# A two-layer decoder trunk on one core: the next norm's weights applied after the transposes, two more pairs by seven products, fewer up blocks added by TensorE, and the issue order as a table

## The chip, the core and the metric

The kernel runs on 1 core of one Trainium2 chip. The metric is the device time of one execution in microseconds (us). Engines are called PE (TensorE), DVE (VectorE), ACT (ScalarE), POOL (GpSimd) and SP (the queue that issues most loads).

## The reference

Two layers over x of 256 tokens by 1024 columns, in float32. Each layer normalises x, projects it, runs two groups of attention heads, projects back, and adds the normalised result to x; then the same around an MLP with a squared ReLU:

```python
for l in range(DEPTH):
    h = _rms_norm(x, g_pre_mix[l])
    parts = jnp.split(h @ w_in[l], split_at, axis=-1)
    ...
    mix = jnp.concatenate([o_nsa, o_fox], axis=-1) @ w_out[l]
    x = x + _rms_norm(mix, g_post_mix[l])
    h = _rms_norm(x, g_pre_mlp[l])
    y = jnp.square(jax.nn.relu(h @ w_up[l])) @ w_down[l]
    x = x + _rms_norm(y, g_post_mlp[l])
```

`_rms_norm(x, g)` is x divided by the root of the mean of its squares in a row, times g by columns. `w_up` is 1024 by 4096, `w_down` 4096 by 1024. `o_nsa` is compressed, windowed and selected attention with gates, `o_fox` attention with forget gates.

## The kernel before

**Rounded products.** A float32 matrix is used as the sum of a high and a low part, both in a rounded float format (F32R) that PE streams at one column per cycle. A product of two matrices is three matmuls (`mm3`, line 811): high by high, high by low, low by high. The high half is a copy on ACT, the low half a difference on DVE (`split`, line 832; for weights `Weights.get`, line 567, and `Weights.pair`, line 614). Weight tiles of 512 KB are loaded on SP's queue into the tile wraw, their halves are whi and wlo; of each, seven buffers rotate (`WBUFS`, `LBUFS`, lines 53 and 55). Some up blocks have another way of splitting, by DMAs that POOL issues (`UPS`, line 57).

**The seams.** After attention and after the MLP, `sandwich` (line 883) closes a half layer for one token tile of 128 rows at a time: squares of the bank on ACT, the factor r (`rsqrt_sum`, line 836), the new x, and, in three of the four cases, the normed input of the next half layer, turned so that columns lie on partitions (`to_xT`, line 866: four transposes into one PSUM bank, then one split of 512 columns). Before, the next norm's weights g are applied by columns ahead of the transposes: `pre_gain` (line 874) makes xo = x g and the product of both weights; mg = bank times that product; mg r + xo, in four parts of 256 columns, is what is transposed. The new x itself is made afterwards (m = bank times g_post; x = m r + x). The weights lie in SBUF as rows copied to all partitions (`load_gains`, line 787, tiles gain0 and gain1). The row factor of the next norm is left out here and multiplied in later, as it is one number for each row.

**The MLP.** The hidden width is 32 blocks of 128. Up block 0 to 3 are made by token (`up0`, line 1672). The other 28 are made transposed, two to a step u, in a loop over u (line 1722). A block is one of two kinds. In `add_block` (line 1626) PE adds all three products into one half of a PSUM bank, 24 matmuls of 256 columns. In `up_block` (line 1616) each high weight multiplies the high and low input at once (`block_products`, line 818: 8 matmuls of 512 columns), the low weight 8 times 256; ACT copies the bank out as y, and DVE adds its halves into h. `SUMMED` (line 60) says for each step of a layer which kind its two blocks are: before, 13 of 14 steps of layer 0 and 11 of layer 1 add on PE.

The down product takes the hidden blocks in pairs, by `PAIRS` (line 65): "N" is a plain two by two block product (two token tiles by two column halves by two hidden blocks: eight products), "S" does it with seven products in the manner of Strassen, with sums of weight blocks (wsum) and of activation blocks (quads) made on DVE, into seven PSUM banks that are put together at the end of the layer. Before, 12 of 14 pairs of layer 0 and 14 of 15 of layer 1 are "S"; the remaining hidden blocks are multiplied plainly at the end (`down`, line 1782).

**The order of the work.** Nothing is issued as the program calls it. A `Recorder` (line 221) keeps every operation, works out dependences, and simulates the engines with costs, due times and buffer counts (`order`, line 326; `schedule`, line 356); then `emit` (line 474) issues the operations in that order, and each engine runs its own in it. 92 ranks found beforehand (`RANKS`, line 66) override the computed ones. All instructions are issued at line 481, so the profile tells them apart by tiles.

Of the kernel before, what the change touches and what calls it, by code (L numbers as in the profile page):

```python
# [18 lines left out]
F32 = mybir.dt.float32  # L19
# [15 lines left out]
LANE = 0.9  # L35
PASSES = 4
LANDING = 3500.0

ADDING, ADDED, CAST = 2600, (5000, 5000), (1870, 2500)
SLACK, LATE = {"vector": 20, "scalar": 20}, 1000  # L40

RAMP = {0: 900, 1: 420}
WAIT = 0.4
WARM = (256, 256, 256, 256, 128)
ENTER, LEAVE = 90, 200
SEQ = [(2, 0), (2, 1), (2, 2), (2, 3), (3, 0), (3, 1), (3, 2), (3, 3)]
EVKEY = 1
FIRSTS = [(k, k + 1) for k in range(8)]
NFIRST = 768
HOLD = 150  # L50
REACH = 40
UPK = 7
TOK, WBUFS, RBUFS = 6, 7, 9
LOAD_LEAD, SPLIT_LEAD, ADD_LEAD, CAST_LEAD = 12, 1, 5, 10
# [5 lines left out]
SUMMED = ("11101111111111", "11011111110101")  # L60
# [4 lines left out]
PAIRS = ("NSSSSSSSSSSSSN", "NSSSSSSSSSSSSSS")  # L65
RANKS = (
# [17 lines left out]
)  # L84
QT = (1, 1)
# [130 lines left out]
class Op:  # L216
    __slots__ = ("small", "engine", "name", "args", "kw", "key", "urgent", "cost", "deps", "succs", "bufs",
                 "missing", "ready", "start", "end", "tile", "rank")


class Recorder:
    def __init__(self, nc, tc):
        self.nc, self.tc = nc, tc
        self.ops, self.stages, self.fifo, self.key, self.hot, self.lane, self.group = [], [], {}, None, False, None, None
        self.after = None
        for e in ("tensor", "vector", "scalar", "gpsimd", "sync"):
            setattr(self, e, _Engine(self, e))
# [15 lines left out]
    def add(self, engine, name, args, kw):  # L243
        if self.group is not None:
            assert engine == "tensor"
            self.group.append((name, args, kw))
            return
        op = Op()
        op.engine, op.name, op.args, op.kw = engine, name, args, kw
        op.key = len(self.ops) if self.key is None else self.key  # L250
        if self.lane is not None and self.key is None:
            op.key = self.lane + LANE * (len(self.ops) - self.lane)
        op.urgent = self.hot
# [4 lines left out]
        op.tile = _tile(op) if engine == "tensor" else None  # L258
        op.small = engine == "tensor" and not any(v.buf.name.startswith(("whi", "wlo")) for _, v in views)
        op.cost = _cost(op, views) + SLACK.get(engine, 0)  # L260
        deps = {} if self.after is None else {self.after: -1e9}
        op.bufs = []
        for is_out, v in sorted(views, key=lambda x: x[0]):
            b, m = v.buf, v.mask()
            if b not in op.bufs:
                op.bufs.append(b)

            def against(entries):
                for o, p, q, bank in entries:
                    if o is not op and o not in deps and (  # L270
                            (bank and engine == "tensor") or
                            (p[0] < v.p[1] and v.p[0] < p[1] and (m & q).any())):
                        deps[o] = _latency(o, op)

            against(b.writes)
            entry = (op, v.p, m, is_out and b.psum and engine == "tensor")
            if is_out:
                against(b.reads)
                b.writes = [w for w in b.writes if not (
                    w[0] in deps and v.p[0] <= w[1][0] and w[1][1] <= v.p[1] and not (w[2] & ~m).any())]  # L280
                b.writes.append(entry)
            else:
                if b.psum:
                    for o, _, _, _ in b.reads:
                        if o.engine != engine and o is not op and o not in deps:
                            deps[o] = 130.0
                b.reads.append(entry)
        op.deps = deps
        for b in op.bufs:
            if not b.ops:  # L290
                self.fifo.setdefault(b.tag, []).append(b)
            b.ops += 1
        op.succs = []
        for d in deps:
            d.succs.append(op)
        self.ops.append(op)

    def deadlines(self, out):


        due, t = {}, 0.0
        for op in out:
            if op.engine == "tensor":
                due[op], t = t, t + op.cost
        taker = {}
        for q in self.fifo.values():
            for a, b in zip(q, q[q[0].bufs:]):
                taker[a] = b
        first = {}
        for op in out:  # L310
            for b in op.bufs:
                first.setdefault(b, op)
        for op in reversed(out):
            d = due.get(op, t)
            cost = op.cost + LANDING if op.engine == "sync" else op.cost
            for x in op.succs:
                if x.deps[op] > -1e8 and x in due:
                    d = min(d, due[x] - x.deps[op] - cost)
            for b in op.bufs:
                if taker.get(b) in first and first[taker[b]] in due:  # L320
                    d = min(d, due[first[taker[b]]] - (260 if b.psum else 150) - cost)
            due[op] = d
        for op in out:
            op.rank = op.key if op.engine == "tensor" else due[op]

    def order(self):

        for op in self.ops:  # L330
            op.rank = op.key
        done = 0
        for bound in self.stages + [len(self.ops)]:
            rest = self.ops[done:]
            best = None
            for first in ([op.rank for op in rest], [op.key for op in rest]):
                for op, rank in zip(rest, first):
                    op.rank = rank
                for i in range(PASSES + 1):
                    if i:  # L340
                        kept = [op.rank for op in self.ops[:done]]
                        self.deadlines(out)
                        for op, rank in zip(self.ops, kept):
                            op.rank = rank
                    out = self.schedule()
                    end = max(op.end for op in out)
                    if best is None or end < best[0]:
                        best = end, [op.rank for op in rest]
# [1516 lines left out]
```

## Time and profile before

| | |
|---|---|
| median of 3 runs | 573.61 us (572.9 to 573.81) |
| profiled execution | span 572.4 us from its first to its last instruction; no other time of its own is listed |
| PE, weight loads | 564.1 us busy (99% of the span), 503.0 (88%) |
| DVE, ACT, POOL | 534.5 (93%), 452.4 (79%), 49.4 (9%) |
| matmuls | 3696 |
| HBM | 133.9 MB read, 236 GB/s over the span |

A group row reads: line, engine, operation, tile written and tiles read, shapes, count, then busy time in us and the mean of one in ns, then idle time of the engine just before them and what ended it. In the rows every line is L481, the line at which all instructions are issued.

### The profile page before, as it was taken

To read this page: it belongs to the slowest core of one execution; us is meant where nothing else is said; L and a number is where in the kernel's file an instruction comes from. 1 tells how busy PE (TensorE), PEld (TensorE's weight loads), DVE (VectorE), ACT (ScalarE), POOL (GpSimd) and SP (SyncE) were. 2 spreads that over 40 slices of the span, in tenths; PEclk is the share of its full clock that TensorE was granted. 3 is DMA by queue.
4 is the path that set the end of the run, shared out by engine and by line. 5 is a ranking of instruction groups with operands and counts; after the bars stand their busy time and mean duration, and the time that the engine had idled before them with its cause. 6 is when DMAs were issued, how large, how long until landed. Compare 5 with 4: busy or idle time off the path is not lost.

```text
span 572.4 us, 10587 instructions
## 1 busy us (share of the span) xinstructions
PE 564.1 (99%) x3696; PEld 503.0 (88%) x3696; DVE 534.5 (93%) x1138; ACT 452.4 (79%) x850; POOL 49.4 (9%) x76
## 2 busy tenths in 40 slices
PE   9999999999999999999999999999999999999995
PEld 7988888789999999999889888878899999999994
DVE  7889899989999999999897899997999999999997
ACT  7898888778987877777569969986879877878873
POOL 0000200011010111000000012000111111111000
PEclk9999999999999999999999999999999999999998
DMA  8988737749999899798438685585498989888621
GB/s 322 380 307 288 272 118 237 261 155 275 289 265 289 252 253 318 196 322 229 143 109 289 251 270 156 182 279 192 142 325 238 299 251 279 259 277 257 144 38 74
DMA packets 39430, 135.69 MB, mean 237 GB/s; under 512 B 4657, under 2 KB 4817, under 8 KB 39377
## 3 DMA queue, kind: packets, MB, share of 16 engines
q1 hardware_dynamic: 31456, 106.17, 52.6%
q0 software_dynamic: 7920, 28.84, 23.0%
q8 instruction: 29, 0.48, 0.3%
q14 instruction: 25, 0.20, 0.1%
HBM read 133.92 MB, written 1.07 MB: 236 GB/s over the span
## 4 chain that ended last, share of the span: by engine, by line
PE 93%; DVE 4%; DMA 1%; ACT 1%; issue 0%; DVEq 0%; ACTq 0%
PE s L481 41%; PE acc L481 21%; PE x L481 20%; PE o L481 11%; DMA wraw<-in_w_in_dram 1%; DVE wlo L481 1%; DVE qS L481 0%; DVE m L481 0%; ACT whi L481 0%; DVE pr L481 0%; DVE x L481 0%; DVE rsqrt L481 0%; ACT qT L481 0%; DVE cs L481 0%; DVE gz L481 0%
## 5 line engine op out<-in xcount | busy, mean ns | idle before, releaser
L481 DVE TENSOR_TENSOR wlo<-wraw,whi 128x1024 fp32r<-128x1024 f32 (+2 forms) x156 | 171.9, 1108 | 10.3 <-ACT whi L481 6.2
L481 ACT ACTIVATE whi<-wraw 128x1024 fp32r<-128x1024 f32 (+2 forms) x165 | 157.9, 966 | 27.9 <-PE s L481 15.6
L481 PE MATMUL s<-xT,whi 128*128 128x256 f32 (+1 forms) x832 | 110.0, 283 | 0.0
L481 PEld LDWEIGHTS s<-xT,whi 128*128 128x128 f32 x832 | 105.2, 192 | 4.5 <-ACT y L481 0.3
L481 ACT ACTIVATE whi<-wsum 128x1024 fp32r<-128x1024 f32 x52 | 54.6, 1056 | 14.4 <-DVE wsum L481 6.0
L481 DVE TENSOR_TENSOR wlo<-wsum,whi 128x1024 fp32r<-128x1024 f32 x52 | 63.2, 1221 | 0.7 <-PE s L481 0.4
L481 PE MATMUL s<-xT,wlo 128*128 128x256 f32 x448 | 59.6, 275 | 0.0
L481 PEld LDWEIGHTS s<-xT,wlo 128*128 128x128 f32 x448 | 56.9, 192 | 1.6
L481 PE MATMUL x<-whi,aS 128*128 128x512 f32 x128 | 47.6, 379 | 0.0
L481 ACT ACTIVATE pr<-pr,st 128x256 f32<-128x256 f32 (+1 forms) x96 | 42.8, 450 | 3.7 <-DVE st L481 3.6
L481 PE MATMUL acc<-whi,aS 128*128 128x512 f32 x128 | 44.7, 380 | 0.0
L481 POOL DMA_DIRECT2D wlo<-in_w_up_dram x31 | 26.8, 865 | 150.9 <-ACT wlo L481 108.5
L481 DVE TENSOR_TENSOR wsum<-wraw,wsum 128x512 f32<-128x512 f32 x52 | 35.7, 686 | 0.1
L481 PE MATMUL s<-whi,aS 128*128 128x512 f32 x104 | 35.4, 380 | 0.0
L481 PE MATMUL acc<-whi,xT 128*128 128x512 f32 (+1 forms) x128 | 35.0, 341 | 0.0
L481 PE MATMUL x<-whi,xT 128*128 128x512 f32 x112 | 34.5, 390 | 0.0
L481 ACT ACTIVATE aS<-quads 128x896 fp32r<-128x896 f32 (+3 forms) x31 | 27.5, 891 | 8.7 <-DVE quads L481 8.2
L481 PE MATMUL acc<-xT,whi 128*128 128x512 f32 x128 | 33.0, 386 | 0.0
L481 DVE TENSOR_TENSOR aS<-quads,aS 128x896 fp32r<-128x896 f32 (+3 forms) x31 | 31.5, 1016 | 0.6 <-ACT aS L481 0.5
L481 DVE TENSOR_TENSOR wsum<-wraw 128x1024 f32<-128x1024 f32 x26 | 31.7, 1220 | 0.0
L481 POOL DMA_DIRECT2D whi<-in_w_up_dram x22 | 12.7, 576 | 203.1 <-PE s L481 71.8
L481 DVE TENSOR_TENSOR quads<-quads 128x128 f32<-128x128 f32 (+1 forms) x81 | 26.8, 335 | 1.2 <-ACT quads L481 0.8
(257 smaller groups left out, 1251.5 us busy)
## 6 DMA issues: line engine op xcount, KB each, us to landing
wraw<-in_w_down_dram SPq DMA_DIRECT2D x64, 512.0 KB, 5.7
wraw<-in_w_up_dram SPq DMA_DIRECT2D x42, 512.0 KB, 5.6
wraw<-in_w_in_dram SPq DMA_DIRECT2D x35, 512.0 KB, 5.2
wlo<-in_w_up_dram POOLq DMA_DIRECT2D x31, 512.0 KB, 7.0
whi<-in_w_up_dram POOLq DMA_DIRECT2D x22, 512.0 KB, 5.3
wraw<-in_w_out_dram SPq DMA_DIRECT2D x16, 512.0 KB, 3.7
w<-in_cmp_w_k_dram SPq DMA_DIRECT2D x8, 512.0 KB, 6.1
w<-in_cmp_w_v_dram SPq DMA_DIRECT2D x8, 512.0 KB, 5.6
```

The costliest lines, as they stand in the source:

```text
L481: getattr(getattr(self.nc, op.engine), name)(*[real(v) for v in args], **{k: real(v) for k, v in kw.items()})
```

## The change

The next norm's weights are no longer applied before the transposes. x itself is updated (in four parts of 256 columns) and transposed; the weights, now one number per partition, come in with the two splits, four pieces of 128 columns each: ACT writes the high part as input times g, DVE the low part as input times g minus the high part. The weights come as columns with an array that is loaded anyway (w2, 16 columns more), so three loads of a gain row and `pre_gain` go. The first products behind a seam take high by high and high by low for four row blocks before low by high. One pair in each layer turns from "N" to "S" (the last of layer 0, the first of layer 1): 28 of 29. 17 steps add their blocks on PE, not 24. The recorder no longer schedules: a table of 5164 entries gives the place of every operation (5200 before).

```diff
-UPK = 7
+UPK = 14
-SUMMED = ("11101111111111", "11011111110101")
+SUMMED = ("11001110111010", "10011110110100")
-PAIRS = ("NSSSSSSSSSSSSN", "NSSSSSSSSSSSSSS")
-RANKS = (
...
+PAIRS = ("NSSSSSSSSSSSSS", "SSSSSSSSSSSSSSS")
+ISSUE = (
...
+        n = len(PLACES)
+        issue = [n * PLACES.index(a) + PLACES.index(b) for a, b in zip(ISSUE[::2], ISSUE[1::2])]
+        assert sorted(issue) == list(range(len(self.ops)))
+        return [self.ops[i] for i in issue]
...
-    def load_gains(*rows):
-        g = [None, None]
-        for i, (name, l) in enumerate(rows):
-            g[i] = tile([P, D], F32, name="gains", tag=f"gain{i}")
-            nc.sync.dma_start(g[i], A[name][l].partition_broadcast(P))
+    def load_gain(name, l):
+        g = tile([P, D], F32, name="gains", tag="gain0")
+        nc.sync.dma_start(g, A[name][l].partition_broadcast(P))
         return g
...
-    def mm3(ps, a, b, start, stop, check=True):
+    def mm3(ps, a, b, start, stop, check=True, passes=(0, 1, 2)):
 
         ps, b = in_turns(ps), [turns(x) for x in b]
-        for j, (u, v) in enumerate(((0, 0), (0, 1), (1, 0))):
+        for j in passes:
+            u, v = ((0, 0), (0, 1), (1, 0))[j]
             nc.tensor.matmul(ps, a[u], b[v], start=start and j == 0, stop=stop and j == 2,
                              skip_group_check=not check)
+
+    def halves_first():
+
+        return [(k, x) for n in (0, 4) for x in ((0, 1), (2,)) for k in range(n, n + 4)]
...
-    def to_xT(t, n, xg, xT):
+    def to_xT(t, n, g, xT):
 
         ps = psum("s")
         with nc.stretch():
             for k in range(4):
-                nc.tensor.transpose(ps[:, k * P:k * P + P], xg[:, k * P:k * P + P], ident)
-        split(ps.rearrange("p (k n) -> p k n", k=4), [y[:, 4 * n:4 * n + 4, t * P:t * P + P] for y in xT[:2]])
-
-    def pre_gain(g_post, g_next):
...
+                nc.tensor.transpose(ps[:, k * P:k * P + P], X[t][:, n * 512 + k * P:n * 512 + k * P + P], ident)
+        into = [[z[:, 4 * n + k, t * P:t * P + P] for z in xT[:2]] for k in range(4)]
+        cols = [(ps[:, k * P:k * P + P], g[:, 4 * n + k:4 * n + k + 1]) for k in range(4)]
+        for (i, c), (hi, _) in zip(cols, into):
+            nc.scalar.activation(hi, i, AF.Copy, scale=c)
+        for (i, c), (hi, lo) in zip(cols, into):
+            nc.vector.scalar_tensor_tensor(lo, i, c, hi.bitcast(F32), op0=OP.mult, op1=OP.subtract)
...
         for n in range(2):
             junk = small([P, 512], "rl")
             nc.scalar.activation(junk, acc[n], AF.Square, scale=1.0 / 32.0, accum_out=sq[:, n:n + 1])
-            if pre:
-                mg[n] = times("mg", n, pre[0])
...
+            if xT or n == 0:
+                times(n)
         r = rsqrt_sum(sq[:, 0:1], sq[:, 1:2], eps, store is not None)
...
-                nc.vector.scalar_tensor_tensor(X[t][:, half(n)], m[n], r, X[t][:, half(n)],
-                                               op0=OP.mult, op1=OP.add)
+                for a in (0, 256) if xT else (slice(0, 512),):
+                    a = slice(a, a + 256) if xT else a
+                    x = X[t][:, half(n)][:, a]
+                    nc.vector.scalar_tensor_tensor(x, m[n][:, a], r, x, op0=OP.mult, op1=OP.add)
...
         yield
+        if xT:
+            for n in range(2):
+                to_xT(t, n, g_next, xT)
+            yield
```

In `up0` and in the first projection of layer 1 (`in_chunk(0, ...)`) the products are called in the order of `halves_first`. The cost functions, due times and ranks of the recorder are removed.

## Rows read from the trace of the kernel before

**Rows 1.** The page, its first part: busy time of the engines.
```profile
span 572.4 us, 10587 instructions
PE 564.1 (99%) x3696; PEld 503.0 (88%) x3696; DVE 534.5 (93%) x1138; ACT 452.4 (79%) x850; POOL 49.4 (9%) x76
```
**Rows 2.** The page, the chain that ended last: shares of the span by engine.
```profile
PE 93%; DVE 4%; DMA 1%; ACT 1%; issue 0%; DVEq 0%; ACTq 0%
```
**Rows 3.** The chain in order of time, three pieces: start us, us, what.
```profile
207.78 2.68 PE s L481 x24
...
538.55 2.62 PE s L481 x16
...
558.14 1.29 PE x L481 x6
```
**Rows 4.** Who waited for whom, PE: us in total, times, longest.
```profile
PE s L481 <- DVE pcs L481: 1.2, 1, 1.2
```
**Rows 5.** Windows, MLP loops: us, busy us of PE, PEld, DVE, ACT, POOL.
```profile
131.00:290.00 159.00, 159.00 (x1055) 148.19 (x1054) 152.86 (x212) 124.65 (x169) 16.51 (x22) 1.00 0.86 250
...
413.00:560.00 147.00, 147.00 (x964) 136.55 (x963) 143.17 (x195) 118.83 (x154) 18.48 (x25) 1.00 0.80 233
```
**Rows 6.** Groups by form, DVE.
```profile
L481 DVE TENSOR_TENSOR wlo<-wraw,whi 128x1024 fp32r<-128x1024 f32 x122 | 148.4, 1222 | 9.9 <-ACT whi L481 6.2 <-PE s L481 1.4 <-ACT wsum L481 0.5
L481 DVE TENSOR_TENSOR wsum<-wraw,wsum 128x512 f32<-128x512 f32 x52 | 35.7, 686 | 0.1
L481 DVE TENSOR_TENSOR wsum<-wraw 128x1024 f32<-128x1024 f32 x26 | 31.7, 1220 | 0.0
L481 DVE TENSOR_TENSOR wlo<-wraw,whi 128x512 fp32r<-128x512 f32 x26 | 17.9, 687 | 0.4 <-PE s L481 0.2
L481 DVE TENSOR_TENSOR quads<-quads 128x128 f32<-128x128 f32 x52 | 14.8, 287 | 0.3
L481 DVE SCALAR_TENSOR_TENSOR x<-m,rsqrt,x 128x512 f32<-128x512 f32 x15 | 10.9, 747 | 0.1
L481 DVE SCALAR_TENSOR_TENSOR mg<-mg,rsqrt,xo 128x256 f32<-128x256 f32 x24 | 10.1, 481 | 0.2
L481 DVE TENSOR_TENSOR xT<-s,xT 128x512 fp32r<-128x512 f32 x12 | 8.2, 688 | 0.3
L481 DVE TENSOR_TENSOR xo<-x,gains 128x1024 f32<-128x1024 f32 x6 | 7.3, 1215 | 0.6 <-PE s L481 0.6
L481 DVE TENSOR_TENSOR m<-x,gains 128x512 f32<-128x512 f32 x8 | 5.3, 685 | 0.3 <-ACT rl L481 0.3
L481 DVE TENSOR_TENSOR gains<-gains 128x1024 f32<-128x1024 f32 x3 | 3.7, 1218 | 0.0
L481 DVE TENSOR_TENSOR h<-y 128x256 f32<-128x256 f32 x8 | 3.4, 420 | 0.0
```
**Rows 7.** Groups by form, ACT.
```profile
L481 ACT ACTIVATE xT<-s 128x512 fp32r<-128x512 f32 x12 | 7.2, 596 | 4.9 <-PE s L481 4.8
L481 ACT ACTIVATE y<-s 128x512 f32<-128x512 f32 x8 | 4.7, 583 | 1.5 <-PE s L481 1.5
L481 ACT ACTIVATE vW<-acc,rsqrt 128x128 f32<-128x128 f32 x4 | 1.5, 364 | 0.0
```
**Rows 8.** Timeline at pcs, layer 0: start us, us, instruction, [idle before, releaser].
```profile
64.86 0.36 PE L481 MATMUL s<-identr,pcs 128*128 128x128 f32 x2 [1.15 <-DVE pcs L481]
```
**Rows 9.** Groups by form, DVE: the scalings of pr in the compressed and windowed attention.
```profile
L481 DVE TENSOR_SCALAR pr<-pr,st,gate 128x256 f32<-128x256 f32 x32 | 13.0, 408 | 0.0
L481 DVE TENSOR_SCALAR pr<-pr,st,gate 128x128 f32<-128x128 f32 x32 | 11.1, 347 | 0.0
```
**Rows 10.** Timeline of PE, from plain transposes back to rounded products.
```profile
93.83 0.46 PE L481 MATMUL x<-whi,oT 128*128 128x512 f32 x1
94.13 0.38 PE L481 MATMUL x<-wlo,oT 128*128 128x512 f32 x1
94.35 0.38 PE L481 MATMUL x<-whi,oT 128*128 128x512 f32 x1
```

More of the change, by code (lines that the diff above doesn't have):

```diff
@@ L84 @@
 )
+PLACES = "".join(chr(c) for c in range(33, 127) if chr(c) not in "\"\\'")
 QT = (1, 1)
@@ L216 @@
 class Op:
-    __slots__ = ("small", "engine", "name", "args", "kw", "key", "urgent", "cost", "deps", "succs", "bufs",
-                 "missing", "ready", "start", "end", "tile", "rank")
+    __slots__ = ("engine", "name", "args", "kw", "bufs")
 class Recorder:
@@ L248, in add @@
         op = Op()
[L249 to L253, printed above, removed]
+        op.engine, op.name, op.args, op.kw, op.bufs = engine, name, args, kw, []
         views = []
@@ L257, in add @@
             views += [(i in ("out", "accum_out"), v) for i, v in k.items() if isinstance(v, View)]
[L258 to L295, printed above, removed]
-        self.ops.append(op)
[L298 to L324, printed above, removed]
@@ L326, in order @@
-    def order(self):
[L330 to L348, printed above, removed]
-            for op, rank in zip(rest, best[1]):
-                op.rank = rank
-            done = bound
-        for i, rank in RANKS:
-            self.ops[i].rank = rank
-        return self.schedule()
@@ L474, in emit @@
+        for _, v in sorted(views, key=lambda x: x[0]):
+            if v.buf not in op.bufs:
+                op.bufs.append(v.buf)
+        self.ops.append(op)
+    def order(self):
+        n = len(PLACES)
+        issue = [n * PLACES.index(a) + PLACES.index(b) for a, b in zip(ISSUE[::2], ISSUE[1::2])]
+        assert sorted(issue) == list(range(len(self.ops)))
+        return [self.ops[i] for i in issue]
     def emit(self):
@@ L512, in _product @@
-def _product(name, args, side):
-    n = int(np.prod(args[0].shape[1:]))
-    rounded = args[1].dtype == F32R
-    if rounded and name != "transpose" and args[2].shape[-1] == 2:
-        return max(112.0, n / 2.4 + 3)
-    if name == "transpose":
-        return 85.0 if rounded else 109.0
-    if side > 1:
-        return n / 2.4 + 20 if rounded else n / 0.6 + (60 if n >= 256 else 11)
-    return max(118.0, n / 2.4 + (14 if n > 256 else 13)) if rounded else max(220.0, n / 0.6 + 7)
-def _cost(op, views):
-    out = op.args[0] if op.args else op.kw["out"]
-    n = int(np.prod(out.shape[1:]))
-    part = 100 * (out.shape[0] < P)
-    if op.engine == "gpsimd":
-        return 200 + 0.72 * n + 10 * int(np.prod(out.shape[1:-1]))
-    if op.engine == "sync":
-        v = views[0][1]
-        run = int(np.prod(v.shape[1:])) * 4 * (1.3 if v.buf.name in ("x0", "x1", "bias") else 1.0)
-        return v.shape[0] * run / 360.0
-    if op.engine == "tensor":
-        if op.name == "stretch":
-            side = P // min(op.tile)
-            return sum(_product(*x[:2], side) for x in op.args[2][::side])
-        return _product(op.name, op.args, 1)
-    if op.engine == "vector":
-        if op.name == "reciprocal":
-            return 60 + 6.5 * n
-        if op.name == "tensor_reduce":
-            n = int(np.prod(op.args[1].shape[1:]))
-        fast = op.name in ("tensor_copy", "tensor_scalar", "memset") and not any(v.buf.psum for _, v in views)
-        aps = sum(isinstance(v, View) for v in op.args[2:4]) if op.name == "tensor_scalar" else int(
-            op.name == "scalar_tensor_tensor" and isinstance(op.args[2], View))
-        return 68 + part + 64 * aps + n * (0.52 if fast else 1.04) + 10 * (op.name == "tensor_tensor_reduce")
-    src = op.args[1]
-    aps = sum(isinstance(op.kw.get(k), View) for k in ("bias", "scale", "accum_out"))
-    return n / 1.2 + (55 if src.buf.psum else 92) + 93 * aps
@@ L585, in get @@
             nc.gpsimd.dma_start(lo, src.bitcast(F32R), accum_op=OP.add)
-            nc.key = None
             return hi, lo
         if i not in self.raw:
-            nc.key = marks[max(i - LOAD_LEAD, 0)]
             self.load(i)
         raw = self.raw.pop(i)
-        nc.key = None
         if kind == "raw":
             return raw
-        nc.key = marks[max(i - (ADD_LEAD if kind == "added" else SPLIT_LEAD), 0)]
         hi = self.tile([P] + shape, F32R, name="whi", tag="whi", bufs=WBUFS)
@@ L761, in trunk @@
         W.raw[k] = f[:, None, o + S:o + NFIRST]
-    nc.after = nc.ops[-1]
     def load_rest():
@@ L768, in trunk @@
     load_rest()
-    nc.after = None
     warm = nc.nc.const_aps.tensor(0.0, [P, S])
@@ L976, in trunk @@
         first = l == 0
-        if not first:
-            nc.stages.append(len(nc.ops))
         if first:
@@ L1242, in in_chunk, with piece @@
             parts = parts_of(l, c)
-            begin = len(nc.ops)
             ps = [None, None]
             ws = {}
-            def piece(t, k, hi, lo, k0):
-                if k == 0:
+            def piece(t, k, hi, lo, k0, passes=(0, 1, 2)):
+                if k == 0 and 0 in passes:
                     ps[t] = psum("o" if by_token and t == 0 else "x" if c in (0, 2) else "acc")
                 mm3(ps[t][:, :n], [y[:, k, t * P:t * P + P] for y in xT[:2]], (hi[:, k - k0, :], lo[:, k - k0, :]),
-                    k == 0, k == 7)
+                    k == 0, k == 7, passes=passes)
             if by_token:
                 for t in range(NT):
-                    for q, (k0, k1) in enumerate(parts):
-                        if t == 0:
-                            ws[q] = weight(l, "in", c, q)
-                        for k in range(k0, k1):
-                            piece(t, k, *ws[q], k0)
+                    for k, x in halves_first():
+                        if k // 2 not in ws:
+                            ws[k // 2] = weight(l, "in", c, k // 2)
+                        piece(t, k, *ws[k // 2], k // 2 * 2, x)
+                        if 2 in x:
                             yield
@@ L1474, in trunk @@
                     urgent(carry)
-                    next(carry)
                     for t in range(NT):
                         r_mix[t] = rsqrt_sum(*squares_of_x(t, "rm"))
+        gains_mlp = par["smT"][:, 38:46]
         row_scales()
@@ L1528, in trunk @@
         if first:
-            nc.after = nc.ops[-1]
             for t in range(NT):
@@ L1581, in urgent @@
         def urgent(gen):
-            nc.hot = True
             next(gen)
-            nc.hot = False
-        steps = [sandwich(t, [accs[t, 0], accs[t, 1]], g_post, pre, xT) for t in range(NT)]
+        steps = [sandwich(t, [accs[t, 0], accs[t, 1]], g_post, gains_mlp, xT) for t in range(NT)]
         out_last(0, 0)
@@ L1676, in up0, with products @@
             q = [None, None]
-            def products(t, ps, k0, k1):
-                for k in range(k0, k1):
+            def products(t, ps, a, b):
+                for k, x in halves_first()[a:b]:
                     if ws[k // 2] is None:
@@ L1682, in products @@
                     w = ws[k // 2]
-                    mm3(ps, [y[:, k, t * P:t * P + P] for y in xT[:2]], [y[:, k % 2, :] for y in w], k == 0, k == 7)
+                    mm3(ps, [y[:, k, t * P:t * P + P] for y in xT[:2]], [y[:, k % 2, :] for y in w], k == 0, k == 7,
+                        passes=x)
             def square(t, ps):
@@ L1703, in up0 @@
             urgent(steps[1])
-            products(0, ps0, UPK, 8)
+            products(0, ps0, UPK, 16)
             square(0, ps0)
-            next(steps[0])
-            next(steps[1])
             ps1 = psum("o")
-            products(1, ps1, 0, 4)
+            products(1, ps1, 0, 8)
             turn(0)
-            products(1, ps1, 4, 8)
+            products(1, ps1, 8, 16)
             square(1, ps1)
@@ L1802, in trunk @@
                     urgent(steps[0])
-                    next(steps[0])
             urgent(steps[t])
```

327 lines of the change are left out of this document (115 added, 212 removed), and 17 rows, old and new, of the table RANKS.

## The prediction

> **What bounds the kernel now.** I read the page first, then the chain of waits, its single pieces, the waits of TensorE, and last the windows and the groups by form for what the other engines have left.
>
> The page shows TensorE (PE) busy for 564.1 of 572.4 us and weight loads for 88% [rows 1]. PE ends are modelled, so busy time alone proves little; the chain gives PE 93% of the span [rows 2], and its pieces give the rate: 24 products of 256 columns follow each other in 2.68 us, 0.112 us each, 6 of 512 columns in 1.29 us, 0.215 each [rows 3]. There are no holes between such pieces to speak of: of all waits of PE inside the run the only one near a microsecond is 1.2 us on the tile pcs in the first layer [rows 4]. So a product taken out is time taken out, as long as nobody else is late. VectorE (DVE) could be: in the MLP loop of the first layer (131 to 290 us) it works 152.9 of 159 us, in that of the second (413 to 560 us) 143.2 of 147 [rows 5]. The kernel is bound by PE, with DVE a few per cent behind it.
>
> A run takes 573.61 us at the median and the profiled span is 572.4, so I count 1.2 us around the span and make the sum against 573.6, which is the median.
>
> **The change, part by part.**
>
> *Two more pairs by seven products.* The last pair of layer 0 and the first of layer 1 go from eight to seven products, each three matmuls of 512 columns. Saved on PE: 2 x 3 x 0.215 = 1.29 us. The price is on DVE. The plain pair splits two tiles of 1024 columns (2 x 1.22); the seven-product pair splits one, half a tile (0.69), makes a sum of 1024 (1.22) and two of 512 (2 x 0.69) and splits two sums (2 x 1.22): 6.94 against 2.44, and two more differences of 128 columns among the activations (2 x 0.29) [rows 6]. That is 5.1 us of DVE a pair, 10.2 in all, beside PE. ScalarE (ACT) makes three high halves more or less in step, about 1.7 us a pair. In layer 0 the pair is now also the closing one, so bank sums that ran under eight products run under the last four of seven, 4 x 0.65 = 2.6 us; three DVE steps of 0.69 fit, and four later products per bank follow.
>
> *Seven up pairs no longer added by PE.* Each has two blocks. An added block is 24 matmuls of 256 columns, 2.68 us; the other form is 8 of 512 and 8 of 256, 2.62 us [rows 3]. Saved on PE: 14 x 0.06 = 0.84 us. For it ACT copies each block out (0.583) and DVE adds halves (0.420) [rows 6, 7]: 8.2 us of ACT and 5.9 of DVE in all, 0.84 of DVE a pair. The copy frees the one PSUM bank that this loop has left for blocks; between two blocks of a pair stand four products, 2.6 us, which cover it.
>
> *The three seams* (after attention in both layers, after the MLP in the first). Out go xo, the product of gains, mg, and its four-part sum: 2 x 1.215 + 1.218 + 4 x 0.685 + 8 x 0.481 = 10.24 us of DVE a seam; the update of x goes from 4 x 0.747 to 8 x 0.481 us (0.86 more), the low halves from 4 x 0.688 to 16 of 128 columns. That form isn't in the trace; the slope between 256 and 512 columns (0.481, 0.747) puts it at 0.35; it lies between the 0.287 of a plain operation of that width and the 0.481 of 256 columns [rows 6]. I take 0.35, the slope's value: 5.6 us, 2.85 more. A seam frees 10.24 - 0.86 - 2.85 = 6.5 us of DVE (4.4 to 7.5 between the bounds). On ACT four copies of 0.596 become 16 scaled ones, for which the nearest row, the same form out of PSUM, has 0.364: 5.8 against 2.4 us, 3.4 more a seam [rows 7]. The transposes wait for x in place of mg, at the same point and behind an equally long sum, so that wait isn't longer; behind them on PE stand the first products, which now take four high parts before the low ones (8 matmuls, 1.7 us, for 4 x 0.364 = 1.46 us of copies). Counted at nothing on PE; if that cover is gone, it is rival C. Three gain loads of 512 KB leave SP's queue, and nothing waits for them: nothing gained.
>
> Sum for DVE: 10.2 + 5.9 - 19.6 = -3.5 us of 534.5; for ACT 3.4 + 8.2 + 10.2 = +21.8 of 452.4 [rows 1]. Neither passes PE over the run.
>
> *The table of the order.* Every queue gets a new order, SP's and POOL's too, and this can cost or give anywhere. Two places can be read off. First the wait on pcs: PE stood 1.15 us at 64.86 until DVE had written pcs [rows 8]. Up to the first gain load the operations carry the same numbers in both kernels, so the table can be laid beside the old order: seven DVE operations that ran ahead of pcs now come behind it, four scalings of pr (2 x 0.408 + 2 x 0.347 = 1.5 us [rows 9]) and three small ones, which I put at 0.2 each, and one scaling of 0.4 comes ahead: pcs is ready 1.5 + 0.6 - 0.4 = 1.7 us sooner. PE comes to these transposes with four matmuls of 512 columns and two of 256 fewer and two of 512 more, 0.65 us sooner. 1.15 + 0.65 - 1.7 is about zero: the wait goes, -1.15 us. Late next are the transposes of the pr that was moved, which have the eight of pcs and three products in front. Second the steps between plain float transposes and rounded products: the first rounded product after one takes 0.30 us before the next starts, in place of 0.22 [rows 10], 0.08 more. The same stretch has 29 steps of this kind in the table against 26: +0.25 us, and I leave the rest of the run at nothing, between -1.7 and +1.
>
> Sum: 573.6 - 1.29 - 0.84 - 1.15 + 0.25 = **570.6 us**.
>
> **Rivals.**
>
> A. *The wait on pcs stays or reappears elsewhere.* For it: my count of what moves is only good to half a microsecond. 570.6 + 1.15 = 571.7.
>
> B. *The order gives more.* Some 42 steps from transposes to rounded products lie in the two layers' attention; half of them gone at 0.08 would be -1.7 us: 568.9. Against it: the part that I can read has more steps, not fewer.
>
> C. *The seams are cut too small.* A transposed bank leaves ACT after 4 x 0.364 = 1.46 us instead of 0.596 [rows 7]. If PE meets that 0.87 us once at each seam: 570.6 + 2.6 = 573.2, no change. For it: ACT is often in a weight copy of 1.05 us when a bank is due. Against it: the new order of products. The rows show about 0.29 us in a copy of 128 columns that isn't for columns (0.596 - 0.364 over 384 columns is 0.6 ns each). The Trainium skill, page VectorE: DVE Perf Modes, section on the errata of SBUF sources, says to tile at 512 elements or more, since each instruction pays a fixed latency again; its ScalarE formula for PSUM (172 + columns, at 1.2 GHz) would give an estimate of 0.25 us, and 4.0 us a seam where I have 5.8.
>
> D. *The products taken out were free.* If PE had slack between products, fewer of them change nothing, and only the wait and the steps count: 573.6 - 1.15 + 0.25 = 572.7. Against it: the spacing of 0.112 and 0.215 us holds through whole blocks [rows 3]. The Trainium skill speaks for it: Perfetto Trace Analysis, section Identifying the Most-Contended Engine, calls matmul busy time a bad measure and wants the busy share of weight loads. That share is 88% here [rows 1], while the spacing leaves no hole; I follow the spacing.
>
> E. *DVE becomes the bound in the MLP loops*, slower. In layer 0 it has 6.1 us idle [rows 5], PE gets 1.1 shorter, and 4 x 0.84 + 5.1 = 8.5 us come in: 3.5 too many unless time freed at the seam carries over. In layer 1: 3.8 idle, 1.0 shorter, 3 x 0.84 + 5.1 = 7.6 in: 4.8 too many. A seam frees 6.5, so about half must carry over in layer 0 and three quarters in layer 1. What carries is work done ahead, and seven low weight tiles of 1.22 us, 8.5 us, can stand ready, so I expect that it does. If only a quarter carries, 1.9 + 3.2 = 5.1 us are lost: 575.7. It decides over no change from 4 us lost on.
>
> **How the numbers follow.** Forecast 0.50, A 0.13, B 0.13, C 0.10, D 0.06, E 0.08. A measurement of this kernel can tell about 0.2%, 1.15 us, from no change, so under 572.5 is faster and over 574.8 slower. Faster: 0.50 + 0.13 + 0.13 = 0.76. Same: C and D, 0.16. Slower: E, 0.08. The range from 568.8 to 573.5 holds all but E and the far half of B; the forecast's own range, from the bounds of the small prices, is 569.8 to 571.4.
>
> **What would show it.** In the changed profile: 34 added blocks and 22 others, so 544 matmuls of 256 columns with a high weight tile into s (768 before) and 176 of 512; 3578 matmuls in all; no PE wait on pcs in layer 0; PE 99% busy, DVE near 531 us, ACT near 474; no gains product, no xo. A is right if PE still waits on pcs or on another tile for about a microsecond; C if PE waits on ACT's xT just behind transposes; E if PE waits on wlo or aS in the loops while DVE is full. The prediction is wrong if the time is under 568.8 with PE products as counted (then the order was worth more than I read) or over 573.5.

## The result and the profile after

The changed kernel takes 580.53 us (median of four runs, 579.94 to 581.65) against 573.25 of the kernel before on the same chip: ratio 1.013, 95% interval 1.0115 to 1.0144. It is slower by 7.3 us, where 570.6 was forecast and the range ended at 573.5. The profiled execution took 580.71 us, 1.8 more than its span.

The page of the changed kernel: its busy line, the granted clock in 40 slices, and the chain by engine.

```profile
PE 564.2 (97%) x3578; PEld 498.2 (86%) x3578; DVE 533.7 (92%) x1169; ACT 473.7 (82%) x904; POOL 49.3 (9%) x76
...
PEclk9999999999999999999999998999999999999999
...
PE 87%; DMA 7%; DVE 2%; ACT 2%; issue 2%; POOL 0%; DVEq 0%; SPq 0%; POOLq 0%; ACTq 0%
```

The work is what was counted: 3578 matmuls, ACT 473.7 us (474 forecast), DVE 533.7 (531). What is new is the chain: PE has 87% of it instead of 93, and DMA 7% instead of 1 [rows 2]. The groups by form agree (the 544 and 176 of the forecast, the 22 copied blocks, the 48 scaled copies of the seams at 0.371 us and their 48 low halves at 0.343, where 0.364 and 0.35 were taken):

```profile
L335 PE MATMUL s<-xT,whi 128*128 128x256 f32 x544 | 83.5, 276 | 0.0
L335 PE MATMUL s<-xT,whi 128*128 128x512 f32 x176 | 46.6, 379 | 0.0
...
L335 ACT ACTIVATE xT<-s,w 128x128 fp32r<-128x128 f32 x48 | 14.4, 371 | 2.4 <-PE s L335 2.3
L335 ACT ACTIVATE y<-s 128x512 f32<-128x512 f32 x22 | 13.1, 594 | 10.7 <-PE s L335 10.4
...
L335 DVE SCALAR_TENSOR_TENSOR xT<-s,w,xT 128x128 fp32r<-128x128 f32 x48 | 14.0, 343 | 0.6 <-ACT xT L335 0.4
```

Who waited for whom on PE (us in total, times, longest) is where the time went. Before, this view had one wait near a microsecond [rows 4]:

```profile
PE s L335 <- DMA wlo<-in_w_up_dram: 4.0, 2, 2.6
PE s L335 <- DVE pcs L335: 1.9, 2, 1.5
PE o L335 <- PEq L1593: 0.8, 1, 0.8
PE s L335 <- DVE st L335: 0.7, 1, 0.7
```

The wait on pcs is gone in layer 0, as forecast, and stands in layer 1 (350.6 us). The largest is on a load. The chain in order of time (start, us, what) has it and the one on pcs:

```profile
245.20 1.18 PE s L335 x10
246.38 11.34 DMA wlo<-in_w_up_dram
257.77 1.16 PE s L335 x8
...
332.16 1.29 DMA sums<-cs
333.59 3.29 DMA bias<-sums
337.21 0.86 POOL bias L335
338.08 2.08 issue
340.19 8.40 DMA whi<-in_w_in_dram
348.67 1.06 ACT wlo L335
350.07 1.23 DVE pcs L335 x2
```

In the first piece POOL's accumulating load takes 11.34 us. SyncE's queue shows what ran beside it: its waits between 228 and 262 us (one of 11.7 us on PE), then what it issued after that wait.

```profile
SPq L335 <- PE s L335: 11.7, 1, 11.7
```

```profile
245.72 0.33 SPq L335 DMA_DIRECT2D gains<-in_g_post_mlp_dram  x1
246.14 6.35 SPq L335 DMA_DIRECT2D wraw<-in_w_down_dram  x6
```

The table puts layer 0's load of the g_post_mlp gains ahead of six weight loads. Its buffer also holds cast weights, and PE frees it late; so SyncE stands still and then sends seven loads while POOL sends its own. The second piece: POOL's load of a weight tile stands behind a mask (affine select) that waits for the forget bias; ACT's negation of that tile stands ahead of the copies of pcs, DVE's subtraction behind those, and PE behind that. Both are places in a queue, not work.

Over the rounded products, the time from one start to the next, added up against the 0.112 and 0.216 us of an undisturbed one of 256 and 512 columns, is 10.5 us late in the kernel before and 19.7 in the changed one: 9.2 more, less 2.13 for removed products, is 7.1. Lateness of over 0.25 us grew from 1.7 to 7.3 us, that of 0.06 to 0.1 us (the steps) from 7.5 to 9.6, that between from 1.8 to 3.3.

### The profile page after: what moved, and what is told of

The parts are those of the page before. It is cut to its first block, busy times and chain, and to the rows that moved or that the text cites. A ratio compares the mean times of both kernels' runs of the same rounds, so it can differ in the third digit from the quotient of the medians.

```text
span 578.9 us, 10437 instructions
## 1 busy us (share of the span) xinstructions
PE 564.2 (97%) x3578; PEld 498.2 (86%) x3578; DVE 533.7 (92%) x1169; ACT 473.7 (82%) x904; POOL 49.3 (9%) x76
## 4 chain that ended last, share of the span: by engine, by line
PE 87%; DMA 7%; DVE 2%; ACT 2%; issue 2%; POOL 0%; DVEq 0%; SPq 0%; POOLq 0%; ACTq 0%
PE s L335 38%; PE acc L335 22%; PE x L335 19%; PE o L335 9%; DMA wlo<-in_w_up_dram 4%; DMA whi<-in_w_in_dram 1%; DVE pr L335 1%; DMA first<-in_first_dram 1%; DMA bias<-sums 1%; ACT whi L335 0%; DVE xT L335 0%; DVE x L335 0%; DVE m L335 0%; DMA sums<-cs 0%; ACT q_tok L335 0%
## 5 line engine op out<-in xcount | busy, mean ns | idle before, releaser
L335 PE MATMUL s<-xT,whi 128*128 128x256 f32 (+1 forms) x720 | 130.1, 301 | 0.0
L335 PEld LDWEIGHTS s<-xT,whi 128*128 128x128 f32 x720 | 111.2, 191 | 8.5
L335 PE MATMUL s<-xT,wlo 128*128 128x256 f32 x448 | 71.2, 275 | 4.0 <-DMA wlo<-in_w_up_dram 4.0
L335 PEld LDWEIGHTS s<-xT,wlo 128*128 128x128 f32 x448 | 65.9, 191 | 8.0 <-DMA wlo<-in_w_up_dram 4.7
L335 DVE TENSOR_TENSOR wlo<-wsum,whi 128x1024 fp32r<-128x1024 f32 x56 | 67.0, 1219 | 1.1 <-ACT whi L335 0.8
L335 ACT ACTIVATE whi<-wsum 128x1024 fp32r<-128x1024 f32 x56 | 58.1, 1053 | 5.9 <-PE s L335 2.8
L335 PE MATMUL x<-whi,aS 128*128 128x512 f32 x120 | 43.3, 380 | 0.0
L335 PE MATMUL s<-whi,aS 128*128 128x512 f32 x112 | 41.4, 380 | 0.0
L335 PE MATMUL acc<-xT,whi 128*128 128x512 f32 x128 | 36.6, 392 | 0.0
L335 ACT ACTIVATE wlo<-whi 128x1024 fp32r<-128x1024 f32 x23 | 24.3, 1055 | 6.8 <-DMA whi<-in_w_in_dram 2.8
```

What stands on the lines that cost most here:

```text
L335: getattr(getattr(self.nc, op.engine), name)(*[real(v) for v in args], **{k: real(v) for k, v in kw.items()})
```

## The experiments

Theory 1: the order in the table costs some 9 us by a few late arrivals, and the arithmetic gives its 2.1 us. Rival: the new arithmetic makes VectorE and ScalarE so full that a wait taken out comes back elsewhere. The first four kernels each move entries of the changed kernel's table; the diffs name the operations.

**The gains' load behind the weight loads.**

```diff
 SyncE, layer 0
-gains <- g_post_mlp
 wraw <- w_down (six loads)
+gains <- g_post_mlp
```

> One entry of the changed kernel's issue table moves: the load of layer 0's g_post_mlp gains goes behind the six weight loads that stood after it on SyncE's queue; nothing else. Changed kernel: 580.5 us. Theory 1 (the table's order): the gains' buffer is free only when TensorE has read the cast weights in it, so SyncE stood 11.7 us (233.6 to 245.7) and then sent seven loads at once beside POOL's accumulating load, which took 11.34 us instead of some 6.5. With the loads spread again that accumulating load takes 5.5 to 7.5 us, TensorE's wait of 2.56 us at 257.8 us is gone, and the time is 577.8 us (577.2 to 578.5). Rival a (the add is late because ScalarE's copy before it is late, 246.4 us): its landing stays 10 to 12 us and the time 580.5. Rival b (the new arithmetic keeps VectorE too busy): this wait goes, but another of 1.5 us or more appears within the next 15 us, and the time stays over 579.7.

Measured: 577.09 us, ratio to the kernel before 1.0067 (1.0046 to 1.0087), 3.6 us under the changed kernel by the ratios. SyncE now issues the six loads over 18 us, and the accumulating load takes 6.4 us (second fence, the DMA view of 244 to 254 us: KB each, median us to landing):

```profile
232.93 17.98 SPq L335 DMA_DIRECT2D wraw<-in_w_down_dram  x6
251.40 0.72 SPq L335 DMA_DIRECT2D gains<-in_g_post_mlp_dram  x1
```

```profile
wlo<-in_w_up_dram POOLq DMA_DIRECT2D x1, 512.0 KB, 6.4
```

The same view of the changed kernel:

```profile
wraw<-in_w_down_dram SPq DMA_DIRECT2D x6, 512.0 KB, 11.2
...
wlo<-in_w_up_dram POOLq DMA_DIRECT2D x1, 512.0 KB, 11.3
```

POOL issued that load at 245.12 us in place of 246.38, hardly sooner, and it landed in 4.9 us less: the burst was the cause, and rival a falls. PE has no wait at that place.

**POOL's load ahead of the masks.**

```diff
 POOL, layer 1
+whi <- w_in (casting load)
 bias <- affine select
-whi <- w_in (casting load)
 bias <- affine select
```

> One entry of the changed kernel's table moves: in layer 1, POOL's casting load of an in_w_in block is issued ahead of the first mask (affine select), as in the kernel before, instead of behind it. Theory 1 (order): the mask waits for the forget bias until 337.2 us and holds the load until 340.2; it lands at 348.6; ScalarE's negation of it stands ahead of the copies of pcs, and TensorE waits 1.64 and 0.60 us for pcs. With the load ahead it lands by 343 us, ScalarE's 2.8 us wait and both of TensorE's go, and so does the stretch of half clock right behind them (about 0.9 us): 577.4 to 578.3 us. Rival a: the load's buffer comes free too late anyway (POOL waited 2.1 us for it), landing and time stay within 0.5 us of 580.5. Rival b: pcs is late through VectorE's own work, the wait of TensorE on pcs stays over 1 us although the load lands early; over 579.7.

Measured: 576.69 us, ratio 1.0064 (1.005 to 1.0078), 3.8 us under the changed kernel and somewhat better than expected. The load is issued at 334.15 us and lands in 4.9 us instead of 8.4; ACT's negation at 346.05 doesn't wait, and PE has no wait on pcs.

```profile
334.15 0.56 POOL L335 DMA_DIRECT2D whi<-in_w_in_dram  x1 [65.60 <-ACT whi L335]
...
337.90 1.61 POOL L335 TENSOR_SCALAR_AFFINE_SELECT bias<-bias 128x256 f32<-128x256 f32 x2 [3.19 <-DVE wlo L335]
```

**Five masks elsewhere.** In the changed kernel PE also waits 0.74 us at 379.2 us. On DVE, a scaling of pr that takes 0.347 us by the group [rows 9] takes 1.60 there, and POOL runs five masks in those same 1.8 us:

```profile
376.78 1.60 DVE L335 TENSOR_SCALAR pr<-pr,st,gate 128x128 f32<-128x128 f32 x1
...
376.81 1.84 POOL L335 TENSOR_SCALAR_AFFINE_SELECT bias<-bias 128x256 f32<-128x256 f32 x5
```

```diff
 POOL, layer 1
-whi <- w_up (casting load, waits for its buffer until 376.2 us)
 bias <- affine select (five times)
+whi <- w_up (casting load)
```

> One entry of the changed kernel's table moves: POOL's casting load that waits for its buffer until 376.2 us goes behind the five masks of layer 1 that stood after it, so the masks run some 20 us earlier. Theory: VectorE's scaling of pr at 376.8 us took 1.60 us instead of 0.34 because those five masks ran on POOL at the same time (376.81 to 378.65), and TensorE waited 0.74 us for what follows it (0.9 us start to start). With the masks elsewhere the scaling at that place takes 0.3 to 0.7 us, TensorE's wait at 379.2 us is gone, and the time is 579.6 us (579.0 to 580.2). Rival: the 1.60 us are VectorE's own (its operand came late); the duration stays over 1.2 us and the time 580.5.

Measured: 582.09 us, ratio 1.0156 (1.0138 to 1.0174): slower than the changed kernel by 1.5 us. The mechanism was right and the sign of the edit wrong. The scaling takes 0.35 us, but the masks, now six in a row, meet the two subtractions of pcs, which take 3.01 us instead of the 1.23 in the chain above, and PE waits for those:

```profile
351.06 3.01 DVE L335 TENSOR_TENSOR pcs<-cs,pcs 128x256 fp32r<-128x256 f32 x2 [2.62 <-ACT pcs L335]
...
377.77 0.35 DVE L335 TENSOR_SCALAR pr<-pr,st,gate 128x128 f32<-128x128 f32 x1
...
351.60 2.72 POOL L335 TENSOR_SCALAR_AFFINE_SELECT bias<-bias 128x256 f32<-128x256 f32 x6
```

The hold follows the masks. The Trainium skill, SBUF — State Buffer, section SBUF: two separate sides, says that VectorE, in a 2-port mode or (against a GpSimd instruction that reads SBUF) with two inputs in SBUF, and GpSimd share a pair of ports under an exclusive lock: whichever starts first has it for the whole instruction, and the other is fully blocked. The trace agrees that one blocks the other. It doesn't agree that the first to start wins: by the profile the scaling started at 376.78 us, the first mask at 376.81. And the scaling, which has one tensor input (in which mode it ran no run shows), lost 1.25 us, more than three masks of 1.84 / 5 = 0.37, so with masks back to back VectorE did not get in after the first.

**Ready products first.**

```diff
 TensorE, layer 0, at 144 us
-eight s <- xT,wlo (in twos among the products below)
 eight acc, x <- aS products of the block before
+eight s <- xT,wlo
```

> In the changed kernel's table, TensorE's eight products with the low half of one up block of layer 0 go behind eight products of the block before (acc and x from aS), which stood between and behind them. Theory: those products wait 1.48 us at 146.0 us for POOL's accumulating load (issued 135.1, landed 146.0, 10.9 us), while some 1.3 us of other work is ready; with it put ahead the gap shrinks to 0.4 us or less and the time is 579.2 us (578.8 to 579.8). Rival: the products put ahead have their own operand late (the subtractions for aS end at 142.5, those for the low halves at 144.8 us), a gap of over 1 us stays in the stretch from 143 to 149 us, and the time is 580.5.

Measured: 579.38 us, ratio 1.0113 (1.0089 to 1.0138). That is 1.0 us under the changed kernel, near the expected time, but the interval overlaps that of the changed kernel (1.0115 to 1.0144), so a gain isn't shown. The gap of 1.64 us at 144.3 us is gone. In the three profiles above, which leave that place alone, it was 0.27 to 0.51 us: most of it is chance in when the load lands.

**Together.** Three of the moves (all but that of the five masks), and then two more: masks two at a time around POOL's load, and nine transposes moved to their neighbours.

```diff
 POOL, layer 1 (the second kernel)
+bias <- affine select (four)
 wlo <- w_in (accumulating load)
 bias <- affine select
+bias <- affine select
 whi <- w_up (casting load)
-bias <- affine select (five)
```

> Three of the moves together on the changed kernel: the gains' load behind the six weight loads, POOL's layer-1 load ahead of the masks, and the eight products of low halves behind ready ones. Theory (the table's order, and the three places independent): alone they stood 3.4, 3.8 and 1.1 us below the changed kernel's 580.5; together some 8 us, less 0.5 to 1.5 that was chance in the single runs: 573.0 us (572.0 to 574.5), against 573.0 of the kernel before. Rival (the new arithmetic keeps VectorE and the queues so full that a wait taken out comes back within the next stage): the sum of TensorE's gaps over 250 ns stays over 4 us and the time is 575.5 or more.

> The three moves, and two more: the five masks of layer 1 that stood in one row on POOL are issued two at a time as their bias comes in, around POOL's next load, as in the kernel before (three runs of masks instead of one of five); and nine of TensorE's transposes are moved next to a neighbour of the same tile, so that the steps between transposes and rounded products fall from 190 to 182 (the kernel before has 158). Theory: the scaling of pr that took 1.60 us takes 0.35 and TensorE's gap of 0.9 us goes, and eight steps fewer at some 0.08 us give 0.6 us: 571.5 us (570.5 to 572.8), 1.5 below the three moves alone and below the kernel before. Rival: the masks hold VectorE where pcs is made, as when all five were moved there (the subtraction of pcs then took 3.0 us instead of 1.2): TensorE waits over 1 us for pcs and the time is 573.5 or more.

Measured: 573.70 us with three moves, ratio 1.0011 (0.9998 to 1.0024); 572.52 with five, 0.9994 (0.9985 to 1.0004). Lateness of PE over 0.25 us is 2.5 us with three moves and 0.35 with five. By the ratios, three moves of table entries take back 6.8 us, less than the 8.4 that the single runs add up to, and five take back 7.8. The rival predicted 575.5 or more and falls.

**The steps alone.** 15 more moves of TensorE's entries, from 182 to 152 changes between transposes and rounded products, counted in the issue order.

```diff
 TensorE
 transposes of pr (one run)
-one to twelve products
 transposes of pr (the next run)
+one to twelve products
```

> The five moves, and 15 more moves of TensorE entries alone: a run of transposes that is parted from the next by one to twelve products is put next to it, so that the steps between transposes and rounded products fall from 182 to 152 (158 in the kernel before, 190 in the changed kernel). Nothing else moves. Theory (such a step costs 0.07 to 0.1 us of TensorE's time, wherever it stands): 30 steps fewer are worth 2.2 us (1.5 to 2.7): 570.3 us (569.8 to 571.0), 2.7 below the kernel before, which is the gain that the arithmetic and the wait on pcs were priced at. Rival (the transposes moved later or earlier make what reads them late, or hold a bank of PSUM longer): TensorE's gaps over 250 ns, 0.35 us in all with the five moves, grow by 1.5 us or more and the time stays within 0.7 of 572.5.

Measured: 572.59 us, 0.9998 (0.9984 to 1.0012), no gain over the five moves. The theory falls, and so does the rival's reason: the gaps over 0.25 us didn't grow. Added up over the two traces, the products' spacing shrank by 1.5 us, but that of the 296 transposes grew by 1.2 (25.8 to 27.0 us). A step that is saved is mostly paid again among the transposes: 0.08 us is where the time is booked, not its price.

**The arithmetic undone, part by part,** on the grouped order.

```diff
-PAIRS = ("NSSSSSSSSSSSSS", "SSSSSSSSSSSSSSS")
+PAIRS = ("NSSSSSSSSSSSSN", "NSSSSSSSSSSSSSS")
```

> The grouped order, with the number of pairs by seven products put back from 28 to 26 as in the kernel before (the last of layer 0 and the first of layer 1 by eight); what replaces an operation stands in its place in the order. Theory (the two pairs are worth 1.29 us of TensorE's time, and nothing else limits): 1.3 us above the grouped order (0.8 to 1.9). Rival (the pairs by seven cost as much in VectorE's and ScalarE's work as they save): within 0.5 us of it.

```diff
-SUMMED = ("11001110111010", "10011110110100")
+SUMMED = ("11101111111111", "11011111110101")
```

> The grouped order, with the pairs of up blocks that TensorE adds put back from 17 to 24 as in the kernel before: 14 blocks by 16 products of 256 columns in place of 8 of 512, without the copies and additions on ScalarE and VectorE that these needed. Theory (TensorE's time is worth what was priced, 0.84 us, and VectorE has room): 0.8 us above the grouped order (0.4 to 1.4). Rival (VectorE is the bound in the MLP's loops, so 14 additions and copies less on it are worth more than TensorE's products): below the grouped order by 0.5 us or more.

Measured: with 26 pairs 575.00 us, ratio 1.0032 (1.0021 to 1.0043), 2.4 above the grouped order; with 24 pairs added by TensorE 573.80, 1.0010 (1.0001 to 1.0018), 1.2 above. So the seven-product pairs help. Their 2.4 us are above the expected range; the profile, of the longest execution, has a wait of 1.7 us on a copy of ACT that may come from where the replaced operations were put. If every execution has it, the pairs themselves are worth 0.7, so 0.7 and 2.4 bound them. Putting back the 24 added pairs frees VectorE and isn't faster: ten of its eleven runs lie above the grouped order's median, though the two intervals overlap, so the 1.2 is at the edge of what can be told. The busy lines of the grouped order, of 26 pairs and of 24 added pairs:

```profile
PE 562.1 (99%) x3578; PEld 497.1 (87%) x3578; DVE 532.2 (93%) x1169; ACT 472.5 (83%) x904; POOL 51.3 (9%) x76
```

```profile
PE 564.3 (98%) x3584; PEld 498.3 (87%) x3584; DVE 523.8 (91%) x1155; ACT 469.5 (82%) x900; POOL 50.7 (9%) x76
```

```profile
PE 563.2 (99%) x3690; PEld 501.3 (88%) x3690; DVE 528.7 (93%) x1155; ACT 465.6 (81%) x890; POOL 51.7 (9%) x76
```

**Second profiles** of the kernel before and of the grouped order, both unchanged (no edit).

> The kernel before itself, unchanged, for a second profile of it. Its first profile spans 572.4 us, which with the 1.8 us around the span is an execution of 574.2, 1.1 above the median of its runs. Theory a (the wait of 1.15 us on pcs in layer 0 belongs to the order of the kernel before): TensorE waits 1.0 to 1.3 us on pcs again, and a span of 571.2 has something else shorter. Theory b (that wait came with that one execution): a profile with a span near 571.2 has no wait of over 0.5 us on pcs, and the term of 1.15 us in the forecast was not there to be won.

> The grouped order unchanged, for a second profile. Its first profile is of its fastest execution, 571.5 us, 1.1 below its median of 572.6; no wait of TensorE over 0.8 us is in it. Theory a (its slower executions differ by a late transfer): a profile of 572.5 us or more shows one or two waits of TensorE on a load or on what a load feeds, 0.5 to 2 us in all. Theory b (they differ by TensorE's clock or by many small steps): such a profile shows no wait over 0.4 us, and the busy time of TensorE is 0.5 to 1.5 us above 562.1.

Measured: 573.42 us (0.9999, 0.9987 to 1.0010) and 572.70 (0.9999, 0.9987 to 1.0011). The second profile of the kernel before, an execution of 573.52 us, has half the wait on pcs; neither of the two theories as put:

```profile
PE s L481 <- DVE pcs L481: 0.6, 1, 0.6
```

The grouped order at 572.75 us shows no wait over 0.4 us once the first product has been issued, and PE busy 562.9, 0.8 more than in its fastest: theory b, many small delays. The two spans, 571.75 and 570.98, differ by 0.8 us.

**Another order for the same arithmetic.** All edits of the change with the planner of the kernel before in place of the table.

```diff
-ISSUE = (... 5164 entries ...)
+RANKS = (... 1368 ranks, searched anew ...)
```

> All arithmetic of the change (the weights on the turned x, 28 pairs by seven, 17 pairs added by TensorE), in an order that the planner of the kernel before makes, with its ranks searched anew for the new operations, but far less long than a tuned order has been; no table. Its steps between transposes and rounded products are 152. By its own reckoning this order ends at 579.3 us and the kernel before at 574.6, which is measured at 573.0. Theory (the order decides, the arithmetic is worth its 2.1 us in each): this order lands by the reckoning's own bias at 577.7 us (576.0 to 579.0), by waits at other places than in the changed kernel. Rival (it was the table alone that was bad; any order of the planner keeps pace): 573.0 us or less.

Measured: 579.90 us, ratio 1.0119 (1.0103 to 1.0136), 0.9 above the expected range. The same work as in the changed kernel, the same time, and other waits:

```profile
PE x L742 <- ACT aS L742: 2.5, 2, 1.7
PE s L742 <- DMA wlo<-in_w_up_dram: 1.6, 2, 0.8
PE s L742 <- DVE pcs L742: 1.3, 1, 1.3
PE x L742 <- DVE oT L742: 1.2, 1, 1.2
```

The profile is of its longest execution, 584.0 us. So the table isn't alone in being badly ordered: between this order and the grouped one, with the same work, lie 7 us, more than the whole arithmetic is worth.

## Why the prediction was wrong

*The step that failed* is the table of the order: "Every queue gets a new order, SP's and POOL's too, and this can cost or give anywhere", and then one stretch of it was priced, +0.25 us, with the rest "at nothing, between -1.7 and +1". The result lies 10.3 us above the forecast (7.3 slower in place of 3.0 faster), and moves of table entries alone take back 7.8 of them: that is what the order cost at the least. The table was at hand: the gains' load ahead of six weight loads and POOL's load behind a mask could both be read off it, with what each waits for. For the bound of +1 the prediction gives no working; the one stretch that it compared is in the attention of layer 0, and the two costliest places lie outside it.

*Two more pairs by seven, seven up pairs not added:* right. Matmul counts are exact; undoing the pairs costs 0.7 to 2.4 us (1.29 priced), undoing the up pairs 1.2, at the edge of the noise (0.84 priced). Rival D falls with the pairs: removed products were not free, so the spacing was the better guide than the busy share of weight loads.

*The wait on pcs:* right for layer 0, where the wait went. Its size was that of one execution: 1.15 us in the first profile, 0.6 in the second. That execution was also longer than the runs: its span of 572.4 and the 1.8 us around it, which later profiles show, make 574.2, not the 573.6 that the sum started from. Rival A named what happened (pcs waits again, in layer 1), but not its cause, POOL's queue.

*The steps:* the count rose (190 against 158 in the issue order) and their lateness by 2.1 us, but 30 fewer gave nothing. Rival B's 1.7 us weren't there.

*The seams:* counted at nothing on PE. The waits of PE in the changed kernel have none on xT, so rival C's mechanism isn't there; no run puts the old seams back, so what they are worth as a whole isn't shown. *VectorE as the bound* (E) falls: in the grouped order it is busy 152.1 of 159 us in the first loop, as before [rows 5], PE is busy throughout, and the kernel that relieves VectorE by 3.5 us over the run isn't faster. The windows of the grouped order:

```profile
131.00:290.00 159.00, 159.00 (x997) 146.54 (x996) 152.12 (x222) 133.94 (x191) 16.06 (x21) 1.00 0.84 251
413.00:560.00 147.00, 147.00 (x918) 135.42 (x917) 144.50 (x201) 123.98 (x163) 18.54 (x25) 1.00 0.79 226
```

*What stays open:* with its order mended, the change comes to 572.5 us, 0.4 under the kernel before and not to be told from it, where the arithmetic alone should give 2.1. The traces show where the rest goes. Take as stage borders the last product that reads oT (end of the projection back) and the last that reads aT (end of the down product). In the pair of first profiles (kernel before, grouped order) the two MLP stages together are 2.7 us shorter, in the pair of second profiles 2.4; some 0.4 of that are four transposes that move into an attention stage, and what is left is about what the arithmetic was priced at, with two of the three new seams in it. The two attention stages together are 0.1 us shorter in the first pair and 1.5 longer in the second, although the wait on pcs (1.2 and 0.6 us) is gone from them. So the arithmetic's gain is there, and the attention stages, whose arithmetic is as before but for the third seam, give it away; whether by their order or by that seam wasn't tried. No version here beats both kernels by more than the measurement can tell.

## What to carry to other kernels

When a change brings a new issue order, read it queue by queue before pricing anything else: for each load that waits for a buffer, what stands behind it on its queue; for each operation that waits for a transfer, what on the critical path is queued behind it. Where arithmetic is worth 2 us, one load in the wrong place is worth 3.6. And take the price of a wait from more than one profile, against that execution's own time.

## What was not expected of the hardware

After a wait of PE of 1.6 to 2.7 us the granted clock in some executions falls to its lower level, 1.2 GHz: at the soonest while PE still waits and at the latest some 2 us after it has started again, and it stays there for 3 to 7 us. It did so five times in four of the profiles (the changed kernel and the first three moves); with the ready products first PE had waits as long, of 1.6 and 2.4 us, and the clock stayed at 2.4 GHz. Windows (us, busy of PE, PEld, DVE, ACT, POOL, then the granted clock) of the changed kernel behind its two waits for pcs, and of the kernel with POOL's load moved, behind a wait of 2.1 us at 255.4:

```profile
348.00:351.00 3.00, 1.41 (x9) 1.02 (x7) 0.93 (x2) 2.33 (x6) 0.98 (x2) 1.00 0.52 210
351.00:353.30 2.30, 1.96 (x13) 1.96 (x14) 2.27 (x7) 2.29 (x8) 0.54 (x1) 0.68 0.77 109
353.40:355.00 1.60, 1.60 (x8) 1.51 (x8) 1.57 (x8) 1.55 (x4) 0.00 (x0) 0.50 1.03 215
```

```profile
253.00:255.40 2.40, 0.55 (x3) 0.14 (x1) 2.40 (x4) 1.59 (x2) 0.00 (x0) 1.00 1.00 362
255.40:257.00 1.60, 1.38 (x10) 1.36 (x11) 0.92 (x1) 0.19 (x1) 0.00 (x0) 1.00 1.02 417
257.00:260.00 3.00, 3.00 (x11) 2.59 (x11) 2.16 (x3) 2.62 (x4) 0.00 (x0) 0.51 0.84 341
```

The products at the lower clock are spaced twice as far: some 1.6 us extra in each of the two kernels, so the second's wait of 2.1 us cost 3.7. The wait of 2.56 us in the changed kernel had no such tail. And one accumulating load of 512 KB took 6.4 us with the six weight loads spread over 18 us, and 11.3 us with seven loads issued in 7 us beside it.
